# Queries and keys of the first heads projected side by side, some of their K tiles by seven products, in a two-layer hybrid decoder trunk

## The chip, the cores and the metric

The kernel runs on one core of a Trainium2 chip. The metric is the device time of one execution in microseconds (us); less is better. Engines are named as in the profile: PE is TensorE's matmul, PEld its weight load, DVE is VectorE, ACT is ScalarE, POOL is GpSimd, SP is SyncE, which issues most loads.

## The reference

Two layers, each on x of 256 tokens by 2048 columns, all in float32:

```python
h = _rmsnorm(x, attn_norm_g[l])
proj = h @ w_in[l]
q, k, v, gate_b, gate_c, conv_in = jnp.split(proj, splits, axis=-1)
q = _rmsnorm(q.reshape(B, S, N_HEADS, 2, HEAD_DK), q_norm_g[l])
k = _rmsnorm(k.reshape(B, S, N_HEADS, 2, HEAD_DK), k_norm_g[l])
...
conv = gate_b * _short_conv(gate_c * conv_in, conv_w[l])
x = x + jnp.concatenate([attn, conv.astype(attn.dtype)], axis=-1) @ w_out[l]
hm = _rmsnorm(x, mlp_norm_g[l]) @ w_up[l]
x = x + jnp.square(jax.nn.relu(hm)) @ w_down[l]
```

Each of the six parts of `proj` is 1024 columns wide. There are 8 heads of 128 value columns, and each head has two maps of 64 query and key columns: attention is the difference of two softmaxes, causal, with a relative bias. `w_up` is 2048 by 8192, `w_down` 8192 by 2048.

## The kernel before

**Number format.** A float32 product is made of three: every operand is split into a high part (ACT copies it, rounded, to the matmul's format) and a low part (DVE subtracts the high part from the whole), and high x high, high x low and low x high are accumulated (`TERMS`). So each weight tile costs one ACT operation and one DVE operation of 128x1024 (lines 328 and 329, tiles `whi` and `wlo`).

**Weights.** `Weights` holds a list of jobs in the order of use. `take()` hands out the next pair of parts, and builds three jobs ahead (`AHEAD`). A job loads 512 KB into one of four `raw` buffers (SP issues the load, line 369) and splits it into one of three `hi` and `lo` buffers. A job is a pair of K tiles (2 x 128 rows) by 512 columns.

**Order of the work.** PE's instructions run in the order of the program text; on the other engines the compiler orders the queue by a plan of its own, except for operations marked `late`, which keep program order. Work that lies beside the matmuls is written as generators in `Background`: every six matmuls or so `work.tick()` counts down their waits, and a piece whose wait is over issues its next operations, its transposes on PE among them. So "yield 12" is twelve ticks later.

**A layer.** `mixer` projects, for each half of the heads, q, k and v with `linear` (line 427): 8 jobs, 2 K tiles each, 2 token tiles, 3 terms, 96 matmuls of 128x512 a projection. `acc` is a tile of two PSUM banks, from a pool of two such tiles (`mm`); a further pool (`ps`) has three banks `bank` and one `av`, eight in all. After q, `qk_norm` (line 617) starts: for each token tile a square on ACT, a sum on DVE, the power on POOL (line 489), and the multiply into `wide` tiles on DVE (line 631); 12 ticks later the result is transposed on PE (line 640) and split by head (`q_parts`, `k_parts`). It runs under k's matmuls, k's norm under v's. `attention` of a half starts after its v and runs under what follows. Then come the convolution's gates (`linear_t`, `conv`), the output projection (`BySeven.left`, `.right`) and the MLP.

**The input norm.** `Norm.chunk` (line 502) transposes 512 columns of x on PE, multiplies by the gain and splits (`split_gained`, lines 294 and 296). There are four chunks, each of four K tiles, so pairs 6 and 7 of the eight pairs are chunk 3. The factors per row come later (`factors`, line 551): they are multiplied into the results, and a matmul with ones, "rbc" at line 578, lays them out along a row for the convolution.

**By seven products.** Two K tiles, two token tiles and two column chunks form a 2x2 by 2x2 block product, which is done here with seven products instead of eight (Winograd's form). `BySeven.sums_of` (line 797) makes the four sums of activations S1 to S4 (four DVE operations of 128x512, one ACT and one DVE to split), `jobs` (line 816) the parts of the weights in three jobs: `plain` loads two raw tiles and splits b11, b21 and b22; `sums` and `more` make and split t1, t3 and t2, t4. A product is three matmuls. Products 2, 3 and 4 go into the ordinary accumulators, 1, 5, 6 and 7 into banks of their own, which are gathered by ACT and DVE at the end (`results`, line 897). The output projection's right half does pairs 2 and 3 that way (order in `RIGHT`, `right()` at line 1003, line 876 for the matmuls), the down projection does 83 pairs (`quarters`, line 1165; `product`, line 1326), where `plain` splits 512 columns as `b1` and 1024 as `b2`.

**Bias.** `load_bias` (line 272) loads the reversed bias rows through POOL's queue (line 280) and copies them on ACT (line 286); in layer 0 it first runs the small setup (gains, lambda).

Of the kernel before, what the change touches and what calls it, by code (L numbers as in the profile page):

```python
# [15 lines left out]
P = 128  # L16
# [28 lines left out]
SEVEN_RIGHT = tuple(i for what, i in RIGHT if what == "s")  # L45

# [82 lines left out]
def trunk(ctx: ExitStack, tc: tile.TileContext, x, w_in, w_out, conv_w, q_norm_g, k_norm_g,  # L129
# [25 lines left out]
    work = Background()  # L155

# [115 lines left out]
    def load_bias(l, bpool, bias, setup):  # L272
# [219 lines left out]
    class Norm:  # L492
# [3 lines left out]
        def __init__(self, which, l):  # L496
            self.which, self.l = which, l
            self.squared = 0
            self.tiles = [Parts(apool, "a", f"nT{which}{l}_{n}") for n in range(D // CH)]
            self.ss = small.tile([P, NT, D // CH], F32, tag="ss", name=f"ss{which}{l}", bufs=2)  # L500

        def chunk(self, n, wait):
# [5 lines left out]
            for j in range(2):  # L508
                tp = bank(f"tpn{n}_{j}")
                for i in range(2):  # L510
                    k = 2 * j + i
                    for t in range(NT):
# [3 lines left out]
                split_gained(a, *((2 * j + i, tp[:, i * S:(i + 1) * S],  # L516
                                   norm_gain(self.which, self.l, n * KG + 2 * j + i))
                                  for i in range(2)))
# [32 lines left out]
        def factors(self):  # L551
# [24 lines left out]
            yield 5  # L576
# [40 lines left out]
    def qk_norm(acc, r, put, gain, name):  # L617

        out_ = []
        for t in range(NT):  # L620
            rt = r[:, t:t + 1]
            sq = wide(f"{name}sq{t}")
            nc.scalar.activation(sq, acc[:, t], AF.Square, scale=rt)
# [6 lines left out]
            qn = wide(f"{name}n{t}")  # L630
            nc.vector.tensor_tensor(
                qn.rearrange("p (g d) -> p g d", d=DK),
                acc[:, t].rearrange("p (g d) -> p g d", d=DK),
# [154 lines left out]
    class BySeven:  # L788
# [3 lines left out]
        def __init__(self, l, bpool, biasp, tmp, weights):  # L792
            self.l, self.pool, self.weights = l, bpool, weights
            self.biasp, self.tmp = biasp, tmp
            self.sums, self.rooms = {}, []

        def sums_of(self, i, a11, a21, a12, a22):

            if i < 4:
                if i % 2 == 0:  # L800
# [15 lines left out]
        def jobs(self, w, i, col):  # L816
# [3 lines left out]
            def split(hi, lo, src):  # L820
                nc.scalar.activation(hi, src, AF.Copy)
                nc.vector.tensor_sub(lo, src, hi.bitcast(F32))
# [7 lines left out]
            def plain():  # L830
                raws = []
                for n in range(2):
# [3 lines left out]
                               col + n * CH:col + (n + 1) * CH].rearrange(  # L836
# [9 lines left out]
            def sums():  # L846
                left, right = mine["raw"]
                pool, tag = (self.pool, "b") if col else (self.kpool, "kL")
# [30 lines left out]
        def pair(self, i, chunks, starts=(), last=False):  # L879

            for n, accs in chunks:
                hi, lo = self.weights.take()
                for j in range(2):
# [4 lines left out]
                    for t in range(NT):  # L888
                        for m, (pa, pw) in enumerate(TERMS):
                            nc.tensor.matmul(  # L890
                                accs[t], a.ap[:, pa, k % KG, t * P:(t + 1) * P],
                                (hi, lo)[pw][:, j],
                                start=(j == 0 and m == 0 and (n, t) in starts),
                                stop=(last and j == 1 and m == 2))
# [22 lines left out]
        def left_jobs(self, w_gate, col, w):  # L917

            weights, made = self.weights, {}
            for what, i in LEFT:  # L920
                if what == "c":
                    weights.jobs += weights.column(w_gate, col + i * P)
                elif what == "a":
                    made[i] = self.jobs(w, i, 0)
# [71 lines left out]
        def right_jobs(self, w):  # L996
            for what, i in RIGHT:
                if what == "s":
                    self.weights.jobs += self.jobs(w, i, 2 * CH)
                else:  # L1000
                    self.weights.plain(w, 2 * P * i, (2 + what) * CH, 2)

        def right(self, norm):
# [7 lines left out]
            def seven(i, start, end, rest):  # L1011
                if start:
                    for n in (1, 5, 6):
                        prods[n] = bank(f"po{l}r{n}")
                    prods[7] = ps.tile([P, CH], F32, tag="av", name=f"po{l}r7", bufs=1)
                b11, b21, b22 = weights.take()
                t1, t3 = weights.take()
                t2, t4 = weights.take()
                for n, a, b, chunk in ((1, A11, b11, None), (2, A12, b21, 0), (3, S4, b22, 1),
                                       (5, S1, t1, None), (7, S3, t3, None), (6, S2, t2, None),  # L1020
                                       (4, A22, t4, 0)):
                    if chunk is None:
                        self.product(n, i, a, b, start, end)
                    else:
                        self.product(n, i, a, b, False, not {"s", chunk} & rest)
                    if n == 5:
                        work.tick()
                work.tick()

            for j, (what, i) in enumerate(RIGHT):  # L1030
                rest = {w for w, _ in RIGHT[j + 1:]}
                if what == "s":
                    seven(i, i == SEVEN_RIGHT[0], i == SEVEN_RIGHT[-1], rest)
# [17 lines left out]
    def mixer(l, norm, loads):  # L1051

        with ExitStack() as scope:
# [9 lines left out]
            for half in range(2):  # L1063
                for part in range(3):
                    weights.straight(w_in[l], 0, D // P, part * AW + half * CH)
# [9 lines left out]
            bias = [biasp.tile([P, NH, S], F32, tag="bias", name=f"bias{j}") for j in range(2)]  # L1075
            work.start(load_bias(l, bpool, bias, setup), 10)
# [6 lines left out]
            for half in range(2):  # L1083
                h0 = 4 * half
                acc = linear(f"q{l}{half}", hT, weights)
                r = norm.r
                qT = bpool.tile([P, 2, 4, S], F32R, tag="b", name=f"qT{l}{half}")
                work.start(qk_norm(acc, r, q_parts(qT), q_gain[:, l:l + 1], f"q{l}{half}"))
                acc = linear(f"k{l}{half}", hT, weights)
                kT = bpool.tile([P, 2, 4, S], F32R, tag="b", name=f"kT{l}{half}")  # L1090
# [521 lines left out]
```

## Time and profile before

| what | value |
|---|---|
| median of 3 runs | 2118.36 us (2118.16 to 2118.75) |
| the profiled execution's own time | 2118.11 us |
| its span, first to last instruction | 2116.0 us |
| granted TensorE clock | 1.00 |
| DMA | 476.02 MB, mean 225 GB/s |
| loads of w_in | 191 of 512 KB, median 4.2 us to landing |

In the profile a group of instructions is given by line, engine, operation and tiles (out<-in). Timeline rows begin with the start in us from the span's start and the duration; several instructions in a row may be merged ("x6"). Rows of the chain in order of time have start, length and what ran. In a row of stages the pairs are busy us and the number of instructions for PE, PEld, DVE, ACT and POOL, then the granted clock, the DMA share and GB/s. Matmuls overlap in the trace (0.39 us each, one started every 0.23), so their pace is read from starts. First q matmul: 6.9 us in layer 0, 1063.1 in layer 1.

### The profile page before, as it was taken

What the parts mean: (1) busy time and instruction counts of PE and PEld (TensorE: products, weight loads), DVE (VectorE), ACT (ScalarE), POOL (GpSimd) and SP (SyncE); (2) the same over time, 40 slices, a digit from 0 to 9 for tenths busy, and PEclk for the clock granted to TensorE, in tenths of its full rate; (3) what the DMA queues carried; (4) which work ended last, traced back from release to release, by engine and by line L of the source; (5) the groups of instructions that cost most, each with busy time, mean ns of one, the idle gap of its engine ahead of it and who ended that gap; (6) DMA issues with size and microseconds to landing.
All of it is one profiled execution on the core that took longest, in us unless ns stands there. A gap on an engine that the chain in (4) does not pass through costs nothing.

```text
span 2116.0 us, 29387 instructions
## 1 busy us (share of the span) xinstructions
PE 2111.2 (100%) x10833; PEld 1804.9 (85%) x10833; DVE 1784.5 (84%) x2519; ACT 1401.8 (66%) x1880; POOL 159.4 (8%) x226
## 2 busy tenths in 40 slices
PE   9999999999999999999999999999999999999999
PEld 8888888888888888888888888888888888888887
DVE  6778788898888888799766788988988888888997
ACT  6777565676776776666566766557777677675664
POOL 3110100000000000011101101000000000000110
PEclk9999999999999999999999999999999999999999
DMA  8555665887777777788656555658877777777993
GB/s 280 175 154 179 186 193 189 288 258 229 236 230 231 229 238 229 248 299 293 213 170 181 165 171 180 207 179 291 258 229 238 230 236 229 231 229 262 318 311 104
DMA packets 313857, 476.02 MB, mean 225 GB/s; under 512 B 12692, under 2 KB 209638, under 8 KB 313713
## 3 DMA queue, kind: packets, MB, share of 16 engines
q1 hardware_dynamic: 285232, 406.76, 61.0%
q0 software_dynamic: 28288, 67.24, 10.0%
q8 instruction: 85, 1.39, 0.3%
q14 instruction: 60, 0.48, 0.1%
q10 hardware_dynamic: 192, 0.15, 0.0%
HBM read 440.52 MB, written 33.58 MB: 224 GB/s over the span
## 4 chain that ended last, share of the span: by engine, by line
PE 99%; ACT 0%; issue 0%; DMA 0%; DVE 0%
PE upc L1286 31%; PE pr L1329 14%; PE dn L1410 8%; PE ci L467 4%; PE gc L467 4%; PE gb L419 4%; PE k L442 4%; PE q L442 4%; PE v L442 4%; PE o L890 3%; PE dn L1504 2%; PE po L876 2%; PE dn L1329 2%; PE pr1r L1329 2%; PE po L890 2%; PE pr0r L1329 1%
## 5 line engine op out<-in xcount | busy, mean ns | idle before, releaser
L1286 PE MATMUL upc<-nT,uhi 128*128 128x512 f32 x1920 | 454.7, 389 | 0.0
L1286 PEld LDWEIGHTS upc<-nT,uhi 128*128 128x128 f32 x1920 | 360.3, 188 | 74.7
L1150 DVE TENSOR_TENSOR ulo<-uraw,uhi 128x1024 fp32r<-128x1024 f32 x256 | 311.9, 1222 | 110.8 <-ACT f L1318 90.8
L328 ACT ACTIVATE whi<-raw 128x1024 fp32r<-128x1024 f32 x246 | 260.0, 1059 | 211.4 <-PE v L442 22.1
L329 DVE TENSOR_TENSOR wlo<-raw,whi 128x1024 fp32r<-128x1024 f32 x246 | 298.5, 1222 | 118.1 <-ACT whi L328 85.7
L1149 ACT ACTIVATE uhi<-uraw 128x1024 fp32r<-128x1024 f32 x256 | 270.6, 1057 | 158.8 <-PE upc L1286 138.9
L1286 PEld LDWEIGHTS upc<-nT,ulo 128*128 128x128 f32 x1920 | 246.2, 191 | 9.3
L1286 PE MATMUL upc<-nT,ulo 128*128 128x256 f32 x1920 | 249.1, 283 | 0.0
L1410 PE MATMUL dn<-whi,fb 128*128 128x512 f32 x496 | 156.5, 389 | 0.0
L1175 ACT ACTIVATE b2h<-draw 128x1024 fp32r<-128x1024 f32 x83 | 88.2, 1062 | 48.5 <-PE pr L1329 39.8
L328 ACT ACTIVATE whi<-uraw 128x1024 fp32r<-128x1024 f32 x62 | 65.9, 1062 | 81.8 <-PE dn L1410 61.0
L1410 PEld LDWEIGHTS dn<-whi,fb 128*128 128x128 f32 x496 | 93.1, 188 | 19.2
L1296 ACT ACTIVATE ev<-upc 128x512 f32<-128x512 f32 x120 | 71.9, 599 | 53.4 <-PE upc L1286 53.4
L1175 ACT ACTIVATE t24h<-t 128x1024 fp32r<-128x1024 f32 x83 | 88.2, 1063 | 22.9 <-PE pr L1329 15.9
L1176 DVE TENSOR_TENSOR t24l<-t,t24h 128x1024 fp32r<-128x1024 f32 x83 | 101.2, 1220 | 1.7
L1176 DVE TENSOR_TENSOR b2l<-draw,b2h 128x1024 fp32r<-128x1024 f32 x83 | 101.1, 1218 | 1.1 <-ACT b2h L1175 1.1
L1176 DVE TENSOR_TENSOR t13l<-t,t13h 128x1024 fp32r<-128x1024 f32 x83 | 101.2, 1219 | 0.7
L1189 DVE TENSOR_TENSOR t<-draw 128x1024 f32<-128x1024 f32 x83 | 101.3, 1220 | 0.3
L1175 ACT ACTIVATE t13h<-t 128x1024 fp32r<-128x1024 f32 x83 | 88.3, 1064 | 13.3 <-DVE t L1189 2.9
L1410 PE MATMUL dn<-wlo,fb 128*128 128x512 f32 x248 | 96.5, 389 | 0.0
L1329 PE MATMUL pr<-t13h,f 128*128 128x512 f32 x240 | 93.8, 391 | 0.0
L329 DVE TENSOR_TENSOR wlo<-uraw,whi 128x1024 fp32r<-128x1024 f32 x62 | 75.8, 1223 | 17.9 <-ACT whi L328 17.6
(491 smaller groups left out, 4428.6 us busy)
## 6 DMA issues: line engine op xcount, KB each, us to landing
uraw<-in_w_up_dram SPq DMA_DIRECT2D x128, 1024.0 KB, 6.3
raw<-in_w_in_dram SPq DMA_DIRECT2D x191, 512.0 KB, 4.2
draw<-in_w_down_dram SPq DMA_DIRECT2D x174, 512.0 KB, 5.2
raw<-in_w_out_dram SPq DMA_DIRECT2D x64, 512.0 KB, 4.5
uraw<-in_w_down_dram SPq DMA_DIRECT2D x62, 512.0 KB, 5.9
raw<-in_w_down_dram SPq DMA_DIRECT2D x10, 1024.0 KB, 5.6
hid0p<-f POOLq DMA_DIRECT2D x19, 512.0 KB, 3.5
fb<-hid0p POOLq DMA_DIRECT2D x19, 512.0 KB, 6.8
```

The source lines that it names most:

```text
L328: pair = (nc.scalar.activation(hi, raw, AF.Copy), nc.vector.tensor_sub(lo, raw, hi.bitcast(F32)))
L329: nc.vector.tensor_sub(lo, raw, hi.bitcast(F32)))
L442: nc.tensor.matmul(acc[:, t], a.ap[:, pa, k % KG, t * P:(t + 1) * P], (hi, lo)[pw][:, j], start=(k == 0 and (pa, pw) == (0, 0)), stop=(k = ...
L467: nc.tensor.matmul(acc[:, f, 0] if part else acc[:, f], wt[:, k % 4, fs], a.ap[:, 0, k % KG] if part else a.ap[:, :, k % KG], start=(part ...
L890: nc.tensor.matmul(accs[t], a.ap[:, pa, k % KG, t * P:(t + 1) * P], (hi, lo)[pw][:, j], start=(j == 0 and m == 0 and (n, t) in starts), st ...
L1149: pair = (nc.scalar.activation(hi, src, AF.Copy), nc.vector.tensor_sub(lo, src, hi.bitcast(F32)))
L1150: nc.vector.tensor_sub(lo, src, hi.bitcast(F32)))
L1175: keep(nc.scalar.activation(hi, src, AF.Copy))
L1176: keep(nc.vector.tensor_sub(lo, src, hi.bitcast(F32)))
L1286: nc.tensor.matmul(acc[:, 0] if part else acc, wt[part][:, k], a.ap[:, 0, k % KG] if part else a.ap[:, :, k % KG], start=(part == 0 and kh ...
L1329: nc.tensor.matmul(prods[n], f[:, pa, a], b[pw], start=(start and m == 0), stop=(stop and m == 2))
L1410: nc.tensor.matmul(prods[p], f[:, pa, 2 * k + t], b[pw][:, n], start=(p in starts and k == 0 and m == 0), stop=(stop and k == 1 and m == 2))
```

## The change

For the first half of the heads, q and k are projected together by `BySeven.first`. It goes through the list `FIRST` of its layer: "(0, i)" is pair i for q, "(1, i)" for k, each 12 matmuls into that projection's two banks; "("s", i)" is pair i for both by seven products. Layer 0 does pair 7 by seven, layer 1 pairs 6 and 7. The products of their own take the three banks and `av`, so all eight are in use; meanwhile (`held`) the bias and the row factors' matmul wait. At the end of the last pair by seven, ACT and DVE gather products 1, 5, 6, 7 into five tiles; when a projection's last pair is done its accumulators are added to these, and `qk_norm` works on the sums in SBUF and multiplies in place. `Norm.chunk` makes the activation sums of those pairs, from a copy of the gained columns (two ACT operations of 256) that is then split at once (512). The weight parts `w7x` and `w7y` use the two `bias` buffers, so the bias tiles are allocated after them. The start of the bias in layer 1 moves from tick 10 to 20, the factors' matmul from 5 ticks behind the factors to 24. `seven` moves out of `right` and is shared. In the down projection, `quarters` splits b11, b21 and b22 in one operation of 1536 columns each on ACT and DVE, which needs the two column halves exchanged; accumulators and additions follow. The second half of the heads and all else stay as they are.

```diff
+FIRST = (((0, 0), (0, 1), (1, 0), (1, 1), (0, 2), (1, 2), (0, 3), (1, 3), (0, 4), (1, 4), ("s", 7), (0, 5), (1, 5), (0, 6), (1, 6)),
+         ((0, 0), (0, 1), (1, 0), (1, 1), (0, 2), (1, 2), (0, 3), (1, 3), ("s", 6), (0, 4), (1, 4), ("s", 7), (0, 5), (1, 5)))
...
+        while held:
+            yield 1
+        bias += [biasp.tile([P, NH, S], F32, tag="bias", name=f"bias{j}") for j in range(2)]
...
+                    y = wide(f"ny{pair}").rearrange("p (k s) -> p k s", k=2)
+                    for i in range(2):
+                        nc.scalar.activation(y[:, i], tp[:, i * S:(i + 1) * S], AF.Copy,
+                                             scale=scales[i])
+                    hi, lo = (a[:, part, 2 * j:2 * j + 2] for part in range(2))
+                    nc.scalar.activation(hi, y, AF.Copy)
+                    nc.vector.tensor_sub(lo, y, hi.bitcast(F32))
+                    self.sums_of(pair, *(y[:, i, t * P:(t + 1) * P]
+                                         for i in range(2) for t in range(NT)))
...
-            yield 5
+            yield 24
+            while held:
+                yield 1
...
-            qn = wide(f"{name}n{t}")
+            qn = acc[t] if in_place else wide(f"{name}n{t}")
...
+                pair = (nc.scalar.activation(hi, src, AF.Copy),
+                        nc.vector.tensor_sub(lo, src, hi.bitcast(F32)))
+                if self.rooms_of == 8:
+                    for ins in pair:
+                        late(ins)
...
+            for j, (what, i) in enumerate(FIRST[l]):
+                rest = {w for w, _ in FIRST[l][j + 1:]}
+                if what == "s":
+                    while not self.cat[2 * i // KG].ready:
+                        work.tick()
+                    held.append(i)
+                    self.seven(i, i == SEVEN_FIRST[l][0], i == SEVEN_FIRST[l][-1], rest)
+                    if i == SEVEN_FIRST[l][-1]:
+                        held.clear()
+                        room = self.tmp.tile([P, 2, CH], F32, tag="ao", name="qe", bufs=1)
+                        e1, e2, e3 = room[:, 0], wide("qe2"), room[:, 1]
+                        e4, e5 = (self.tmp.tile([P, CH], F32, tag="s", name="ke", bufs=2)
+                                  for _ in range(2))
+                        nc.scalar.activation(e1, prods[1], AF.Copy)
+                        nc.vector.tensor_add(e2, prods[6], e1)
+                        nc.vector.tensor_add(e4, prods[5], e2)
+                        nc.vector.tensor_add(e3, prods[7], e2)
+                        nc.vector.tensor_add(e5, prods[5], e3)
+                        e = ((e1, e3), (e4, e5))
+                else:
+                    starts = [(what, t) for t in range(NT) if what not in opened]
+                    opened.add(what)
+                    self.pair(i, [(what, accs[what])], starts, not {"s", what} & rest)
+                for n in list(left):
+                    if not {"s", n} & rest:
+                        for t in range(NT):
+                            nc.vector.tensor_add(e[n][t], accs[n][t], e[n][t])
+                        done(n, e[n])
+                        left.remove(n)
...
-            work.start(load_bias(l, bpool, bias, setup), 10)
+            work.start(load_bias(l, bpool, biasp, bias, setup), 20 if l else 10)
...
-                    h1, l1 = parts(raw[:, 0, 0], "b1", 1)
-                    h2, l2 = parts(raw[:, 1], "b2", 1)
-                    return (h1, l1), (h2[:, 0], l2[:, 0]), (h2[:, 1], l2[:, 1])
+                    raw = mine["raw"] = load_rows(i, col).rearrange("p k (n c) -> p (k n) c", n=2)
+                    h, lw = parts(raw[:, 1:4], "b", 1)
+                    return tuple((h[:, m], lw[:, m]) for m in (0, 2, 1))
...
-                    for n, t, p in ((0, 0, 2), (0, 1, 4), (1, 0, 3), (1, 1, 8)):
+                    for n, t, p in ((1, 0, 2), (1, 1, 4), (0, 0, 3), (0, 1, 8)):
```

More of the change, by code (lines that the diff above doesn't have):

```diff
@@ L1009, in right @@
             opened, add = set(), None
[L1011 to L1028, printed above, removed]
             for j, (what, i) in enumerate(RIGHT):
@@ L1062, in mixer @@
                 setup = setup_loads(bpool.tile([P, 2 * KG * S], F32, tag="b", name="setup"))
-            for half in range(2):
-                for part in range(3):
-                    weights.straight(w_in[l], 0, D // P, part * AW + half * CH)
+            qk_first = BySeven(l, bpool, biasp, tmp, weights, 8)
+            qk_first.cat = norm.tiles
+            norm.sums_of = qk_first.sums_of
+            qk_first.first_jobs(w_in[l])
+            for half, part in ((0, 2), (1, 0), (1, 1), (1, 2)):
+                weights.straight(w_in[l], 0, D // P, part * AW + half * CH)
             for q in range(AW // WC):
@@ L1386, in seven_onto @@
             def seven_onto(n):
-                x11, x21, x12, x22 = (xs[n + i][:, t] for i in range(2) for t in range(NT))
+                x11, x21, x12, x22 = (xs[n + 1 - i][:, t] for i in range(2) for t in range(NT))
                 e1, e2, e3, e4 = wide("e1"), wide("e2"), wide("e3"), wide("e4")
```

122 lines of the change are left out of this document (84 added, 38 removed).

## The prediction

> **What bounds the kernel now.** I read the page first, then who waited for whom on PE, then the chain of work in order of time around the first heads of each layer.
>
> ```profile
> span 2116.0 us, 29387 instructions
> PE 2111.2 (100%) x10833; PEld 1804.9 (85%) x10833; DVE 1784.5 (84%) x2519; ACT 1401.8 (66%) x1880; POOL 159.4 (8%) x226
> PE 99%; ACT 0%; issue 0%; DMA 0%; DVE 0%
> PE warm L183 <- DVE mhalf L175: 1.1, 1, 1.1
> ```
>
> The third line is the chain that ended last: it is PE throughout. The fourth is the whole answer on PE's waits: one wait of 1.1 us, before anything is computed. So PE never waits, and the time is the number of matmuls times their pace. A change pays here only by having fewer matmuls, and costs only by making PE wait. A busy PE need not be at its pace, so I check that in the stage that is changed and in the stage that already works by seven products.
>
> ```profile
> 1086.52 16.32 PE k L442 x72
> ```
>
> ```profile
> 355.83 0.84 PE L876 MATMUL po0r<-w7b,cat 128*128 128x512 f32 x3
> ...
> 359.23 0.84 PE L876 MATMUL po0r<-w7y,sf 128*128 128x512 f32 x3
> ...
> 360.59 0.39 PE L890 MATMUL o<-whi,cat 128*128 128x512 f32 x1
> ```
>
> The k projection of layer 1: 16.32 us / 72 = 0.2267 us for a 128x512 matmul. One pair of K tiles by seven in the output projection goes from 355.83 to 360.59, 4.76 us for 21 matmuls: 0.2267 as well. Both forms run at the same pace, without gaps.
>
> The profiled execution took 2118.11 us with a span of 2116.0, so 2.11 us lie around the span and stay. It is 0.25 below the median of the runs shown (2118.36). All sums below are made against 2118.11; against the median everything is 0.25 higher.
>
> **What the change removes.** A pair of K tiles for one chunk is 2 tiles x 2 token tiles x 3 terms = 12 matmuls; for q and k together 24. By seven products it is 7 x 3 = 21. Layer 0 does one such pair, layer 1 two: 3 x 3 = 9 matmuls less, 9 x 0.2267 = **2.04 us**. Every other matmul and transpose stays, some in another place. PE is never covered by anything, so these 2.04 us come off the end if no new wait appears: 2116.07. The question is whether DVE, ACT and the banks let PE go through.
>
> **What it adds on DVE.** I take start-to-start distances in a full queue:
>
> ```profile
> 328.22 0.69 DVE L907 TENSOR_TENSOR es<-po,e 128x512 f32<-128x512 f32 x1
> 328.82 0.68 DVE L908 TENSOR_TENSOR x<-po,x 128x512 f32<-128x512 f32 x1
> ...
> 611.00 1.22 DVE L1319 TENSOR_TENSOR f<-h,f 128x1024 fp32r<-128x1024 f32 x1
> 612.13 1.22 DVE L1150 TENSOR_TENSOR ulo<-uraw,uhi 128x1024 fp32r<-128x1024 f32 x1
> ```
>
> 0.60 us for 512 columns, 1.13 for 1024. A pair by seven needs three lo parts of 1024, one of 512 and four sums of 512: 3 x 1.13 + 5 x 0.60 = 6.4 us, in place of two plain lo parts (2.26): 4.1 more. The sums of its activations are five operations of 512, 3.0 us. Collecting the products (four operations) and adding them to the accumulators (four): 4.8 us a layer. Norming in place has as many operations as before. Where two gained lo parts of 256 (an estimated 0.35 each, by the same rows) become one of 512, 0.1 goes. Layer 1: 2 x 4.1 + 2 x 3.0 + 4.8 - 0.2 = 18.8 us; layer 0: 4.1 + 3.0 + 4.8 - 0.1 = 11.8.
>
> ```profile
> 22.00:45.00 23.00, 23.00 (x105) 18.21 (x104) 16.30 (x31) 13.87 (x26) 5.63 (x8) 1.00 0.80 275
> 45.00:77.00 32.00, 32.00 (x150) 26.52 (x149) 20.50 (x25) 23.23 (x32) 7.56 (x6) 1.00 0.62 183
> 1063.00:1085.00 22.00, 22.00 (x103) 18.17 (x101) 12.70 (x20) 11.38 (x17) 1.52 (x3) 1.00 0.60 170
> 1085.00:1099.00 14.00, 14.00 (x63) 11.62 (x62) 9.70 (x12) 10.52 (x15) 3.66 (x4) 1.00 0.67 194
> 1099.00:1124.00 25.00, 25.00 (x115) 20.70 (x115) 16.53 (x20) 14.16 (x17) 3.67 (x4) 1.00 0.62 186
> ```
>
> The columns are PE, PEld, DVE, ACT, POOL. Layer 1 has 12.70 + 9.70 + 16.53 = 38.9 us of DVE in 61; with 18.8 more, 57.7 in about 59.6, or 97%. Layer 0: 36.8 + 11.8 = 48.6 in 54, 90%. So in layer 1 DVE comes to within 2 us of the stage's length. Does the kernel already hold that somewhere?
>
> ```profile
> 346.00:367.00 21.00, 20.40 (x28) 1.00 0.63 196
> ```
>
> ```profile
> 356.48 1.22 DVE L822 TENSOR_TENSOR w7y<-w7t,w7y 128x1024 fp32r<-128x1024 f32 x1
> ```
>
> Yes: in the output projection's two pairs by seven DVE is busy 20.40 of 21 us (97%), and PE does not wait; the last part w7y is done at 357.7, 1.5 us before its first matmul at 359.23. That is 21 us and not 60, but the new stage spreads the load: the activation sums are asked for early in layer 1 and needed only 20 us later.
>
> How late may a split be?
>
> ```profile
> 1081.12 1.06 ACT L328 ACTIVATE whi<-raw 128x1024 fp32r<-128x1024 f32 x1 [1.66 <-PE q L442]
> ```
>
> ```profile
> 1082.21 1.23 DVE L329 TENSOR_TENSOR wlo<-raw,whi 128x1024 fp32r<-128x1024 f32 x1 [1.50 <-ACT whi L328]
> ```
>
> A split starts when PE gives back one of three buffers, two groups of 12 (2.72 us each) before the k group at 1086.52 that uses it, and is done at 1083.44: 3.1 us of cover. I count DVE's work by deadline in layer 1, from the first q matmul on. The first pair by seven comes after eight groups of 2.72 us and a little over 0.8 of transposes, its product 5 at 24.6. By then DVE owes six splits (6.8), the row factors (1.0), chunk 3 (1.2), one set of sums (3.0) and the pair's b, t and x parts (4.1): 16.1 of the 23.1 us it has from 1.5 on. At the second pair's last part the same count gives 30.1 of 34.7, at the k transposes about 55 of 58. No deadline is missed; the last one is close.
>
> **Norms side by side.** Both norms now start within 2.7 us and run under v.
>
> ```profile
> 1090.32 1.64 POOL L489 TENSOR_TENSOR q_r<-q_e,mhalf 128x8 f32<-128x8 f32 x1
> ```
>
> Four of these are 6.6 us of POOL, in 16.3 us (12 ticks of six matmuls) from the end of a projection to its transposes: hidden.
>
> ```profile
> 1103.85 2.79 ACT L597 ACTIVATE qT<-q10tp,q_gain 64x512 fp32r<-64x512 f32 x4
> ```
>
> On ACT these four head splits of q (0.70 us each) and the eight of k now follow each other, and layer 1's eight bias copies (512 columns, at most as long: 5.6) move 10 ticks later, beside the squares. ACT has 10.84 us free of 25 in the last row of the windows, where q's splits stand already; the bias fits. If that cover went, PE would wait at a transpose, 1 to 3 us. What else is moved: the two reversed-bias loads of layer 1 on POOL's queue go from tick 10 to 20, behind the row factors and ahead of the norms' powers, and are needed at tick 32 or later; the broadcast of the row factors (0.43 us on PE) moves, its readers come in the convolution. SP issues the same bytes in another order; the pair by seven holds two of the four raw buffers until its last sum.
>
> ```profile
> 359.38 0.69 DVE L851 TENSOR_TENSOR w7t<-raw 128x512 f32<-128x512 f32 x1 [0.55 <-DMA raw<-in_w_out_dram]
> ```
>
> That cost DVE 0.55 us in the output projection and PE nothing. I take nothing for all these; the upper bound is in the rivals.
>
> **The banks.** The pair by seven fills all eight banks, and v's accumulator is q's old one. Its nearest row is the end of the output projection:
>
> ```profile
> 370.56 0.68 DVE L906 TENSOR_TENSOR e<-po0r,es 128x512 f32<-128x512 f32 x1
> ...
> 376.43 1.29 DVE L1044 TENSOR_TENSOR x<-o,x 128x512 f32<-128x512 f32 x2 [0.40 <-PE o L890]
> ```
>
> Four collecting operations of 0.60 begin as the last product ends; two adds begin 0.40 us after their group's end and take 1.2. In the new code k's last group (2.72 us) lies between q's end and v's start: 1.6 us of adds fit with 1.1 to spare, just one split (1.13) between them. Below zero this cannot go: PE had no wait here to lose.
>
> **The down projection's merged split.** 83 times a 512 and a 1024 split become one of 1536, behind product 3.
>
> ```profile
> 604.54 1.06 ACT L1175 ACTIVATE b2h<-draw 128x1024 fp32r<-128x1024 f32 x1 [0.74 <-PE pr L1329]
> ...
> 938.09 1.06 ACT L1175 ACTIVATE b2h<-draw 128x1024 fp32r<-128x1024 f32 x1 [0.41 <-PE dn L1329]
> ```
>
> ```profile
> 618.16 0.40 PE L1329 MATMUL pr<-b1h,f 128*128 128x512 f32 x1
> ...
> 946.05 0.39 PE L1329 MATMUL pr0r<-b1h,fb 128*128 128x512 f32 x1
> ```
>
> From b2h's start my estimate is 1.5 us on ACT and 1.7 on DVE, so it is ready near 607.9 and 941.5, 10 and 4.5 us before use. No cost; and as PE does not wait there, no gain either. The exchange of the two column halves changes no count.
>
> **The sum.** 2118.11 - 2.04 = 2116.07, plus a wait. The unknown wait lies between 0 (the output projection, the nearest row) and 5.3 (rival 2). I take 0.6, half a split late at layer 1's k transposes, where DVE has least to spare: **2116.7 us**. What a measurement can tell from no change is about 0.2%, 4.2 us: the whole expected gain is half of that.
>
> **Rivals.**
>
> 1. *The evacuation takes the place of what was saved.* If two splits stand in DVE's queue before q's adds, v waits 1.6 + 2.26 - 2.72 = 1.1 us in each layer: 2116.07 + 2.3 = **2118.4**, no change. For it: a queue in fixed order, 97% load. Against: the rows at 376.43. The Trainium skill, Perfetto Trace Analysis, section Matmuls, advises letting matmul groups rotate through different PSUM banks so that evacuating one overlaps the next group; taking all eight banks for two projections speaks against this change. The trace before, with the same eight banks in use at 355 to 371, shows no wait, so by the trace it holds only if the adds are late.
>
> 2. *DVE's order makes the splits late (slower).* The place is layer 1 after chunk 3 of the norm: two sums of 3.0 us and two 0.60 lo parts, 7.2 us, ahead of one split with 3.1 us of cover: 4.1 us. In layer 0 one sum, one lo part and the chunk's two gained ones: 3.0 + 0.6 + 0.7 - 3.1 = 1.2. Together 5.3: **2121.4**, slower by 3.3. It decides from the point where more than 3.1 us of other work stands ahead of a split. Against it: needed late, they can be placed late.
>
> 3. *More than counted goes.* Only half as many norm chunks are asked for at a given time, so the start of each layer is less tight. PE shows no wait there, only a slower pace at the kernel's start:
>
> ```profile
> 6.98 4.46 PE q L442 x18
> ...
> 12.32 5.46 PE q L442 x24
> ```
>
> 18 matmuls are 4.08 us at 0.2267, so 0.38 is lost there, and 0.02 in the next 24: **2115.7** if all of it came back.
>
> 4. *The change doesn't pay at all*: something else paces the stage, and 2118.1 stays. Against it is PE's empty list of waits.
>
> **How the numbers follow.** Forecast (2115.9 to 2117.7): 0.60. Rival 1, with late norms (2117.7 to 2119.5): 0.18. Rival 2 (2119.5 to about 2124): 0.14. Rival 3: 0.04. Rival 4: 0.04. The range 2115.6 to 2121.2 leaves out part of rivals 2 and 3, some 0.1. Faster by over 0.2% (under 2114.1) needs more than all that is known to be lost here: 0.02. Slower by over 0.2% (over 2122.6) is rival 2 with the same lateness more than once: 0.08. Within: 0.90.
>
> **What would show it.** Right: PE's list of waits stays near 1.1 us, q and k run at 0.2267, and the first v matmul follows k's last by 0.23 us in both layers. Rival 1 shows as a PE wait at v's first matmul on an add; rival 2 as PE waits on wlo, w7x or w7y with DVE busy before them. A PE wait at the k transposes on the norm's multiply would be the 0.6. I am wrong if the down projection's pairs wait for their b part, or if PE shows no wait and the time is still off by over 1 us.

## The result and the profile after

| | before | after |
|---|---|---|
| median (lowest to highest) of 22 runs each, same chip | 2118.66 us (2118.0 to 2119.53) | 2121.35 us (2119.56 to 2123.46) |
| ratio, 95% interval | | 1.0013 (1.0007 to 1.0019) |
| the profiled execution's own time | 2118.11 us | 2121.82 us |
| its span | 2116.0 us | 2120.1 us |

The changed kernel is slower by 2.7 us, 0.13%. The forecast was 2116.7, the range ended at 2121.2. The head of the page of after, then the whole answer on PE's waits (us in total, times, longest):

```profile
span 2120.1 us, 29191 instructions
PE 2110.3 (100%) x10824; PEld 1802.1 (85%) x10824; DVE 1803.7 (85%) x2482; ACT 1395.7 (66%) x1811; POOL 162.1 (8%) x226
```

```profile
PE q L449 <- DVE wlo L336: 2.1, 2, 1.1
PE k L919 <- DVE wlo L336: 1.4, 1, 1.4
PE warm L187 <- DVE mhalf L179: 1.1, 1, 1.1
PE gb L426 <- ACT gb L798: 0.6, 1, 0.6
PE q L919 <- ACT whi L361: 0.4, 1, 0.4
PE po0r L902 <- DVE w7y L845: 0.3, 1, 0.3
```

PE has its 9 matmuls fewer (10833 to 10824), and where before only the wait at "warm" stood, five more stand now. Three of them are for a low part from DVE (`wlo`, `w7y`).

To place the loss, the span is cut at the first matmul of each stage on PE, read from the timeline of both traces. All stages not in the table (k and v of the second heads, the convolution, the output projection, both MLPs) agree within 0.02 us.

| stage, from first matmul to first matmul (us) | before | after | after less before |
|---|---|---|---|
| up to the first q matmul | 6.91 | 6.76 | -0.15 |
| layer 0, first heads: q, k, v | 72.18 | 72.85 | +0.67 |
| layer 0, second heads: q ("q01") | 24.20 | 25.17 | +0.97 |
| layer 0, gate beside the output projection ("gb") | 84.82 | 85.11 | +0.29 |
| layer 1, first heads: q, k, v | 68.63 | 69.01 | +0.38 |
| layer 1, second heads: q ("q11") | 24.17 | 25.16 | +0.99 |
| layer 1, gate ("gb") | 84.81 | 85.69 | +0.88 |

The sum is +4.03; PE's last matmul starts 4.04 us later than before (the 0.01 left is in the stages not shown). The execution's own time grew by only 3.71: around the span lie 2.11 us before and 1.72 after. The first heads hide what they saved: 3 matmuls (0.68 us) in layer 0 and 6 (1.36) in layer 1. So they lost 1.35 and 1.74 us, the second heads' q 0.97 and 0.99, the gate stages 1.17 together.

**The first heads.** In layer 1, the timelines of PE, ACT, DVE and POOL of after:

```profile
1086.75 0.50 PE L919 MATMUL k<-wlo,nT 128*128 128x512 f32 x1 [1.43 <-DVE wlo L336]
```

```profile
1079.75 1.06 ACT L335 ACTIVATE whi<-raw 128x1024 fp32r<-128x1024 f32 x1 [1.71 <-PE q L919]
```

```profile
1084.27 0.69 DVE L877 TENSOR_TENSOR w7t<-raw 128x512 f32<-128x512 f32 x1 [4.97 <-DMA raw<-in_w_in_dram]
1084.88 0.69 DVE L878 TENSOR_TENSOR w7t<-raw 128x512 f32<-128x512 f32 x1
1085.48 1.22 DVE L336 TENSOR_TENSOR wlo<-raw,whi 128x1024 fp32r<-128x1024 f32 x1
```

Read them from the bottom up. PE waits 1.43 us for a plain pair's `wlo`. Its input, the `whi`, was ready at 1080.81 (1079.75 + 1.06). But DVE's queue holds two sums of the pair by seven ahead of it, and the first of these waits for its load: DVE stands idle for 4.97 us with ready work behind. The load is late because of what was issued beside it:

```profile
1070.57 1.87 POOL L284 DMA_DIRECT2D rev<-by_dist_d  x2 [1.69 <-PE tpn L521]
```

```profile
q0 software_dynamic: 504, 1.93, 48.9%
q1 hardware_dynamic: 814, 1.57, 36.9%
...
raw<-in_w_in_dram SPq DMA_DIRECT2D x3, 512.0 KB, 7.6
```

The second fence is the DMA view of 1074 to 1085 us: the reversed-bias rows (two loads of 1 MB on POOL's queue, q0) move 1.93 MB while SP's queue q1, with the weights, moves 1.57, and a weight load takes 7.6 us. The same window of before has no q0:

```profile
q1 hardware_dynamic: 1059, 2.04, 62.2%
...
raw<-in_w_in_dram SPq DMA_DIRECT2D x4, 512.0 KB, 3.7
```

There the bias loads had gone out before the layer began:

```profile
1035.28 1.82 POOL L280 DMA_DIRECT2D rev<-by_dist_d  x2 [5.05 <-issue]
```

The Trainium skill, DMA: Bandwidth & Descriptors, section Issuing engines are not separate DMA queues, says that transfers started from different engines run on the same 16 DMA engines and interleave. The rows agree: with POOL's queue active, a load on SP's queue takes 7.6 us in place of 3.7 (the median of three loads, and of four). Layer 0 shows the same pattern: DVE's `w7t` there waits 2.91 us for its load, beside bias loads issued at 26.39. PE shows it as the wait of 0.29 for `w7y` and a few gaps of under 0.5 around the pair by seven.

```profile
33.59 0.69 DVE L877 TENSOR_TENSOR w7t<-raw 128x512 f32<-128x512 f32 x1 [2.91 <-DMA raw<-in_w_in_dram]
```

**The second heads' q.** ACT in layer 1 of after, at the last of k's head splits, and PE:

```profile
1129.65 0.68 ACT L631 ACTIVATE kT<-k10tp,gains 64x512 fp32r<-64x512 f32 x1
...
1134.54 0.69 ACT L632 ACTIVATE kT<-k10tp,gains 64x512 fp32r<-64x512 f32 x1
1135.24 2.01 ACT L335 ACTIVATE whi<-raw 128x1024 fp32r<-128x1024 f32 x2
```

```profile
1138.08 0.50 PE L449 MATMUL q<-wlo,nT 128*128 128x512 f32 x1 [1.06 <-DVE wlo L336]
```

Two plain `whi` stand behind eight head splits of k (5.6 us), and q's four came just before those, with one `whi` between. The hi parts, the lo part behind them and PE are late: 1.06 us of wait. Before, q's head splits lay 20 us earlier, under k's projection (they end at 1106.64, k's begin at 1126.55). k's eight stood in the same place as now, and the hi parts behind them began at

```profile
1132.13 2.01 ACT L328 ACTIVATE whi<-raw 128x1024 fp32r<-128x1024 f32 x2
```

That is 0.36 us after the first q11 matmul (1131.77), and the gap on PE was 0.25. In after it is 1.32 us behind it (1133.92): 0.96 later, and the stage is 0.99 longer.

### The profile page after: what moved, and what is told of

It is laid out like the page before. It is cut to its first block, busy times and chain, and to the rows that moved or that the text cites. A ratio compares the mean times of both kernels' runs of the same rounds, so it can differ in the third digit from the quotient of the medians.

```text
span 2120.1 us, 29191 instructions
## 1 busy us (share of the span) xinstructions
PE 2110.3 (100%) x10824; PEld 1802.1 (85%) x10824; DVE 1803.7 (85%) x2482; ACT 1395.7 (66%) x1811; POOL 162.1 (8%) x226
## 4 chain that ended last, share of the span: by engine, by line
PE 96%; DMA 1%; ACT 1%; DVE 1%; issue 1%; POOL 0%; ACTq 0%; DVEq 0%; POOLq 0%
PE upc L1376 31%; PE pr L1419 14%; PE dn L1500 8%; PE ci L474 4%; PE gc L474 4%; PE gb L426 4%; PE v L449 3%; PE o L919 3%; PE dn L1594 2%; PE dn L1419 2%; PE k L449 2%; PE q L449 2%; PE po L902 2%; PE pr1r L1419 2%; PE po L919 2%; PE pr0r L1419 1%
## 5 line engine op out<-in xcount | busy, mean ns | idle before, releaser
L335 ACT ACTIVATE whi<-raw 128x1024 fp32r<-128x1024 f32 x240 | 253.5, 1059 | 194.0 <-issue 20.6
L336 DVE TENSOR_TENSOR wlo<-raw,whi 128x1024 fp32r<-128x1024 f32 x240 | 290.7, 1221 | 90.2 <-ACT whi L335 58.0
L1266 ACT ACTIVATE bh<-draw 128x1536 fp32r<-128x1536 f32 x83 | 123.9, 1493 | 97.6 <-PE pr L1419 80.7
L1267 DVE TENSOR_TENSOR bl<-draw,bh 128x1536 fp32r<-128x1536 f32 x83 | 146.0, 1758 | 12.0 <-ACT bh L1266 11.3
L1419 PE MATMUL pr<-bh,f 128*128 128x512 f32 x360 | 121.4, 391 | 0.0
```

Of the source, the lines that this page charges most:

```text
L335: pair = (nc.scalar.activation(hi, raw, AF.Copy), nc.vector.tensor_sub(lo, raw, hi.bitcast(F32)))
L336: nc.vector.tensor_sub(lo, raw, hi.bitcast(F32)))
L1266: keep(nc.scalar.activation(hi, src, AF.Copy))
L1267: keep(nc.vector.tensor_sub(lo, src, hi.bitcast(F32)))
L1419: nc.tensor.matmul(prods[n], f[:, pa, a], b[pw], start=(start and m == 0), stop=(stop and m == 2))
```

## The experiments

Three edits to the changed kernel take one suspected cost each: K puts k's head splits 3 ticks later, R1 puts layer 1's bias loads ahead of the layer, R0 puts layer 0's setup and bias loads 6 ticks later. Each ran alone and in all combinations. Each of the twelve kernels of this part ran 11 times, beside the kernel before; the interval of one ratio is about 0.0009 to each side, 1.9 us. So the medians alone don't separate single cures, and each verdict also goes by the stage's length in the profile, which for an undisturbed stage repeats to 0.05 us.

| kernel | median us | ratio to before, 95% interval | first heads' q and k, layer 0 / 1 | q01 / q11 |
|---|---|---|---|---|
| before (2118.66 to 2118.86) | | | 49.48 / 45.92 | 24.20 / 24.17 |
| after | 2121.35 | 1.0013 (1.0007, 1.0019) | 48.73 / 45.34 | 25.17 / 25.16 |
| all plain | 2120.79 | 1.0010 (1.0001, 1.0019) | 48.11 / 44.98 | 25.20 / 25.17 |
| all plain, K | 2118.11 | 0.9996 (0.9987, 1.0005) | 48.09 / 44.98 | 23.79 / 23.80 |
| before, merged split only | 2118.11 | 0.9998 (0.9989, 1.0007) | 49.48 / 45.92 | 24.20 / 24.17 |
| before, q beside k | 2120.61 | 1.0009 (1.0000, 1.0018) | 48.55 / 44.98 | 25.18 / 25.17 |
| K | 2118.94 | 1.0002 (0.9993, 1.0011) | 48.76 / 44.41 | 23.82 / 23.80 |
| R1, copies late | 2121.48 | 1.0015 (1.0006, 1.0024) | 48.59 / 43.62 | 25.17 / 26.21 |
| R1 | 2120.38 | 1.0009 (1.0000, 1.0017) | 49.53 / 43.62 | 25.18 / 25.19 |
| R0 | 2121.80 | 1.0013 (1.0004, 1.0022) | 47.40 / 45.38 | 25.18 / 25.20 |
| K, R1 | 2118.57 | 1.0001 (0.9992, 1.0010) | 49.59 / 43.61 | 23.82 / 23.80 |
| K, R0 | 2117.48 | 0.9995 (0.9986, 1.0004) | 47.38 / 43.80 | 23.82 / 23.80 |
| R0, R1 | 2119.06 | 1.0002 (0.9993, 1.0011) | 47.74 / 43.62 | 25.15 / 25.21 |
| K, R0, R1 | 2116.28 | 0.9987 (0.9978, 0.9996) | 47.63 / 43.62 | 23.81 / 23.80 |

In the fourth column the rows "before" and "merged split only" don't compare with the others: elsewhere q's transposes lie under v and not under k, 0.95 us in each layer.

### All pairs plain

```diff
-FIRST = (((0, 0), ... ("s", 7), (0, 5), (1, 5), (0, 6), (1, 6)), (... ("s", 6), (0, 4), (1, 4), ("s", 7), ...))
+FIRST = (((0, 0), (0, 1), (1, 0), (1, 1), (0, 2), (1, 2), ... (0, 6), (1, 6), (0, 7), (1, 7)),) * 2
-                            nc.vector.tensor_add(e[n][t], accs[n][t], e[n][t])
+                            nc.vector.tensor_copy(e[n][t], accs[n][t])
```

> The changed kernel with all eight pairs of K tiles of both layers' first heads plain (no pair by seven; q and k side by side, norms in place, order of the work and the merged split as changed). It issues 9 matmuls more than the changed kernel, as many as the kernel before. Theory A (three separate losses: the pairs by seven lose 2.7 us at the first stages because their raw loads land late; k's head splits standing right behind q's on ACT lose 1.9 us at the stages of q01 and q11; the gate stages lose 0 to 1.2): the time before plus 1.9 to 3.1, that is 2120.6 to 2121.8, with PE's waits at the first q and k stages for wlo gone and the one at q01 (1.2 us) still there. Rival B (DVE or ACT is simply overloaded by the sums of the pairs by seven, and all losses come from there): 2118.4 to 2119.0, and the loss at q01 goes too.

Measured 2120.79. PE's waits for the pairs by seven are gone, and the one at q01 and q11 stays to the last digit:

```profile
PE q L449 <- DVE wlo L336: 2.1, 2, 1.1
```

```profile
PE q L448 <- DVE wlo L335: 2.1, 2, 1.1
```

The first is after, the second all plain (its lines are shifted by one). So the loss at q01 and q11 has nothing to do with the seven products; it comes with side by side alone. Theory A holds, rival B falls.

### The down projection's part alone

```diff
-                    h1, l1 = parts(raw[:, 0, 0], "b1", 1)
-                    h2, l2 = parts(raw[:, 1], "b2", 1)
+                    h, lw = parts(raw[:, 1:4], "b", 1)
```

> The kernel before with only the down projection's part of the change (one split of 1536 columns in place of 512 and 1024, and the column halves exchanged). Theory: no part of the 2.7 us comes from it: 2118.7, within 0.4 of the kernel before. Rival: it delays the pairs by seven of the MLP or the evacuation at its end: 2119.2 or more.

Measured 2118.11, and both MLP stages have the length of before (681.11 and 677.53 us). The merged split costs nothing. The median is 0.67 under that of before beside it (2118.78), more than the 0.4 expected; half of that is the time around the span, which is 1.77 us here and 2.11 before (means over the runs).

### Layer 1's bias loads ahead (R1), in two forms

```diff
-            work.start(load_bias(l, bpool, biasp, bias, setup), 20 if l else 10)
+            work.start(load_bias(l, bpool, biasp, bias, setup), 0 if l else 10)
-        yield 4 if l else 12
+        yield 32 if l else 12
```

> The changed kernel with layer 1's reversed-bias loads issued at the layer's start (before the row factors on POOL's queue, as in the kernel before), the bias copies kept at tick 32. Theory (the two loads of 1 MB each collide with the raw loads of the pair by seven, which then land 3 us late, and DVE's queue stands behind them): PE's wait for wlo in layer 1's first stage goes, the first stage of layer 1 gets 1.3 to 1.7 us shorter, 2119.6 to 2120.1 in all. Rival (the four raw buffers or DVE's own load set the pace, and the loads' collision is a bystander): 2121.0 to 2121.7, with the wait still there.

Measured 2121.48: as the rival had it, though the stage did what the theory said. Layer 1's q and k took 43.62 us and not 45.34, PE's wait there was gone, but q11 went from 25.16 to 26.21. The cause was the edit: with 32 ticks the bias copies came later than in the changed kernel, right ahead of q's head splits on ACT (layer 1):

```profile
1124.55 1.14 ACT L293 ACTIVATE bias<-rev 128x512 f32<-128x512 f32 x2
1125.60 2.78 ACT L619 ACTIVATE qT<-q10tp,q_gain 64x512 fp32r<-64x512 f32 x4
```

The second form has `yield 24 if l else 12`, which leaves ACT's order as changed.

> The earlier experiment with layer 1's reversed-bias loads ahead, mended: there the bias copies had come 8 ticks later than in the changed kernel and pressed on q's head splits on ACT; here they stand where the changed kernel has them, and ACT's order is the changed kernel's. Theory (in the earlier run the first stage's gain of 1.72 us was given back by those copies at q11, 1.05 us, the rest being the landing of the gate stages' loads, which differs from execution to execution): the first stage of layer 1 is 43.6 us, q11's stage is again 25.1 to 25.2, 2119.5 to 2120.2 in all. Rival (whatever is won in the first stage is lost behind it, because the loads and not the splits set the pace of the layer): 2121.0 to 2121.8.

Measured 2120.38, a little above the theory's band and below the rival's; first heads 43.62, q11 25.19, as the theory said. With the loads gone, the pair's own load landed in 4.1 us (the window of 1074 to 1085 again):

```profile
q1 hardware_dynamic: 837, 1.60, 45.3%
...
raw<-in_w_in_dram SPq DMA_DIRECT2D x4, 512.0 KB, 4.1
```

All five kernels with the loads ahead have 43.61 or 43.62 in layer 1, which is the all-plain stage less 6 matmuls: 44.98 - 1.36 = 43.62. The kernels without it have 45.34, 44.41, 45.38 and 43.80. So the collision costs 0.2 to 1.8 us, as the loads happen to land, and moving the loads takes away all of it. The size follows from DVE's wait at `w7t`: it is 4.97, 4.04, 4.99 and 3.42 us in these four kernels, and each time 3.2 us more than what the stage lost (1.72, 0.79, 1.76, 0.18). With the loads ahead the wait is 1.7 to 1.8 us and costs nothing. So about 3.2 us of lateness is covered, as the prediction had read from the trace before (3.1).

### k's head splits later (K)

```diff
-        yield 12
+        yield wait          # 15 for k of the first half, else 12
-                                     1 + half, by_seven.sums_of), 1 + 9 * half)
+                                     1 + half, by_seven.sums_of), 1 + 9 * half + 3 * (half == 0))
```

> The changed kernel with k's transposes and head splits for the first half 3 ticks later, in both layers, so that other hi parts stand between q's four head splits and k's eight on ACT (the attention of that half starts 3 ticks later as well). Theory (twelve head splits in a row delay a plain pair's hi part, and PE loses 1 us in each of the two stages q01 and q11): those two stages get 0.8 to 1.0 us shorter each, 2119.4 to 2119.8 in all. Rival (the loss there is what the first stages' lateness has left over, or the head splits only move the wait into the stage after): 2121.0 to 2121.8.

Measured 2118.94, below the theory's band, and q01 and q11 at 23.82 and 23.80. Now, on ACT in layer 1, a plain hi part stands in the middle of k's eight:

```profile
1132.21 0.69 ACT L632 ACTIVATE kT<-k10tp,gains 64x512 fp32r<-64x512 f32 x1
1132.92 1.06 ACT L335 ACTIVATE whi<-raw 128x1024 fp32r<-128x1024 f32 x1
1134.01 0.69 ACT L1186 ACTIVATE v<-v,rowf 128x512 fp32r<-128x512 f32 x1
1134.59 0.67 ACT L631 ACTIVATE kT<-k10tp,gains 64x512 fp32r<-64x512 f32 x1
```

The stages are 1.35 us shorter, not the 0.8 to 1.0 expected; 0.3 a layer of that only moves to the stages behind (the convolution grows by 0.2, v by 0.1).

### The converse: before, with q's head splits beside k's

```diff
-                work.start(qk_norm(acc, r, q_parts(qT), q_gain[:, l:l + 1], f"q{l}{half}"))
+                work.start(qk_norm(acc, r, q_parts(qT), q_gain[:, l:l + 1], f"q{l}{half}",
+                                   12 if half else 26))
```

> The converse: the kernel before with q's transposes and head splits of the first half 14 ticks later, so that ACT's order there is the changed kernel's (four of q, one hi part, eight of k, two hi parts); nothing else of the change. Theory: the stages q01 and q11 lengthen from 24.2 to 25.1 or 25.2 us each, 2120.4 to 2120.9 in all (before plus 1.9). Rival (the loss at q01 and q11 belongs to the side-by-side order or to the pairs by seven): 2118.6 to 2119.2 and those stages at 24.2.

Measured 2120.61; q01 25.18, q11 25.17, and the wait of after stands in a kernel that has nothing else of the change:

```profile
PE q L442 <- DVE wlo L329: 2.1, 2, 1.1
```

### All plain, with K

The first experiment's edit and K together.

> The all-plain kernel of the first experiment (no pair by seven in the first heads, 9 matmuls more than changed) with k's head splits 3 ticks later. Theory (the neighbourhood of q's and k's head splits on ACT is all that side by side costs without the pairs by seven): 2120.79 less 1.9, that is 2118.5 to 2119.2, the time of the kernel before. Rival (something else of the new order costs as well): 2119.8 to 2120.9.

Measured 2118.11, at the time of before and 0.4 under the band's lower end. So the head splits' neighbourhood is all that side by side costs.

### Layer 0's setup and bias loads later (R0)

```diff
-            work.start(load_bias(l, bpool, biasp, bias, setup), 20 if l else 10)
+            work.start(load_bias(l, bpool, biasp, bias, setup), 20 if l else 16)
```

> The changed kernel with layer 0's small setup and its two reversed-bias loads started 6 ticks later (tick 16 in place of 10), so that they no longer go out beside the raw loads of the pair by seven at 25 us. Theory (the collision delays those loads by 3 us, and PE pays 1.1 us for it in layer 0): the first stage of layer 0 (first q to first v) gets 0.5 to 1.0 us shorter than its 48.7 us, 2120.4 to 2120.9 in all. Rival (the lateness there has another cause, such as the start's own loads): stage unchanged within 0.2, 2121.0 to 2121.7; or the loads collide with the next raw loads, and the wait only moves.

The stage did what the theory said (47.40 in place of 48.73), the median didn't: 2121.80, above the theory and just above the rival's band. By itself this run decides nothing. The stage repeats in the three combinations below: 47.38, 47.74, 47.63, against 48.59 to 49.59 in the five kernels with the pair by seven and the loads as changed.

### The combinations

> The changed kernel with two cures: layer 1's reversed-bias loads ahead (bias copies where they were) and k's transposes and head splits of the first half 3 ticks later in both layers. Theory (the two losses are separate and add): 2118.94 less 1.7, that is 2116.9 to 2117.6, faster than the kernel before by 1 to 2 us. Rival (they share one cause, so the second cure brings nothing): 2118.6 to 2119.3.

Measured 2118.57, at the edge of the rival's band; the stages, however, have both gains (43.61, and 23.82 and 23.80).

> The changed kernel with k's head splits 3 ticks later (both layers) and layer 0's setup and reversed-bias loads 6 ticks later; layer 1's loads as changed. Completes the combinations of the three cures. Theory (three separate losses): 2118.94 less 1.0 to 1.3, that is 2117.4 to 2118.2, with layer 0's first stage at 47.4 to 47.7 us and layer 1's q11 stage at 23.8. Rival (the later loads of layer 0 bring nothing by themselves, as the one run with them alone, 2121.80, says): 2118.7 to 2119.5.

Measured 2117.48, as the theory had it; layer 0's first heads at 47.38, q11 at 23.80.

> The changed kernel with both layers' reversed-bias loads moved (layer 0 later, layer 1 ahead), k's head splits as changed. Theory: the kernel with all three cures (2116.28) plus the 1.9 us of the head splits: 2117.9 to 2118.6, first stages at 47.4 to 47.7 and 43.6 us. Rival (the cures help only together): 2119.5 or more.

Measured 2119.06, between theory and rival.

> The changed kernel with all three cures: layer 1's reversed-bias loads ahead, k's head splits 3 ticks later, and layer 0's setup and reversed-bias loads 6 ticks later. Theory (three separate losses of 1.7, 1.9 and 0.5 to 1.0 us): 2116.0 to 2117.0, which is what the 9 matmuls fewer (2.04 us) leave of the kernel before, with 0 to 0.4 us of waits and some lateness of the gate stages' loads. Rival: as the run with two cures or slower.

Measured 2116.28, ratio 0.9987 (0.9978 to 0.9996): faster than both kernels. With the eight combinations, each cure can be averaged over four kernels with and four without it: K 2117.82 against 2120.65, **-2.8 us**; R1 2118.57 against 2119.89, **-1.3**; R0 2118.66 against 2119.81, **-1.2**. The sum is 5.3, the whole step from after to all three 5.07. That the three losses add is not shown by these sums, in which the effect of one cure on another cancels, and single medians scatter (R0 is +0.45 by itself and -2.29 beside K and R1). It is shown by the stages: each cure shortens its own stage with the others or without them. In the stages from the first q matmul to the gate, the kernel with all three is 2.17 us shorter than before (245.32 against 245.90 and 240.71 against 242.30). That this is near the 2.04 us of the 9 matmuls is luck: all plain with K, which has as many matmuls as before, is already 0.49 shorter than before (245.65 and 242.06), its q01 and q11 being 0.4 shorter each. The pairs by seven give the other 1.68.

## Why the prediction was wrong, point by point

**Right: what is removed.** 9 matmuls, at 0.2267 us each. Beside all plain with K, which has q and k side by side as well, the kernel with all three cures is 1.35 us shorter in layer 1 (6 matmuls are 1.36) and 0.33 in layer 0 (3 are 0.68); in the profile with K and R0, layer 0 is 0.70 shorter.

**Not quite right: "PE never waits."** The list of waits has nothing for before at q11, but its timeline has the gap of 0.25 there. The kernels with K bring q01 and q11 0.4 us under those of before.

**Failed: "I take nothing for all these."** Two of the things costed at nothing were the loss.

- *The bias loads.* The prediction listed them ("the two reversed-bias loads of layer 1 on POOL's queue go from tick 10 to 20") and asked only when they were needed ("at tick 32 or later"; the copies that read them are started at tick 24). It should have asked beside what they would now run: 2 MB in the 10 us in which the pair by seven's first loads are due. It quoted a row of such a load being late by 0.55 us at no cost; here DVE stood 4.97 us. Measured: 1.3 us over the combinations. In layer 0 the loads were not moved; the pair by seven moved beside them, 1.2 us more.
- *ACT's head splits.* "ACT has 10.84 us free of 25 ...; the bias fits" is an average over 25 us. The next plain hi part is due within about 3 us, and stood behind 5.6 us of k's head splits with q's just ahead. The text had the price of a lost cover (1 to 3 us), but looked for it at a transpose; it was at the first low part of the next projection, 1.0 a layer by the stages, 2.8 in all by the combinations (of which before had 0.4 a layer as well).

**Failed: "2.11 us lie around the span and stay."** After has 1.76 on average, and so (1.76 to 1.80) has every kernel with the merged split, also where it stands alone; before and "before, q beside k" have 2.10. This gain of 0.3 hid a part of the loss. The runs do not show why. The least difference that a measurement can tell was also put too high: the interval above is 0.06% to each side, not 0.2%.

**The 0.6 at layer 1's k transposes** did not show: no such wait is in the list.

**Rival 1 (the evacuation) fell.** In both layers v's first matmul follows k's last by 0.23 us (55.49 after 55.26, 1110.25 after 1110.02), as the prediction's own sign asked. q's adds were ready with 0.8 us to spare:

```profile
1108.79 0.68 DVE L1097 TENSOR_TENSOR qe<-q,qe 128x512 f32<-128x512 f32 x1
```

They end at 1109.47, v begins at 1110.25. So taking all eight banks, which the prediction held against the change, cost no wait here.

**Rival 2 gave the time (2121.4 against 2121.35), but not for its reason.** It expected splits late behind 7.2 us of DVE work. Its sign was "PE waits on wlo ... with DVE busy before them"; the waits are there, but in layer 1's first heads DVE was idle before the late part, waiting for a load, and the loss at q01 and q11, 1.96 us by the stages, began on ACT. Its size was wrong as well. The sums of activations (and the text on the kernel before) are not operations of 128x512:

```profile
1071.77 0.28 DVE L834 TENSOR_TENSOR sv<-ny 128x128 f32<-128x128 f32 x1
1071.97 0.28 DVE L832 TENSOR_TENSOR sv<-ny 128x128 f32<-128x128 f32 x1
```

That is 0.20 us from start to start and not 0.60, so a set takes 4 x 0.20 + 0.60 = 1.4 us and not 3.0. The rival's 7.2 us become 4.0, 0.9 over the cover, nothing is left of it in layer 0, and its time becomes 2117.0: that 2121.4 came out is luck. Nor was DVE's load the limit. In the kernel with all three cures, the same 61 us of layer 1 have DVE busy for 52.28 (third pair of the row, after PE and PEld), 86%, where the prediction counted 57.7 and 97% (3.2 of the difference are the two sets of sums); and PE is busy all through:

```profile
1063.00:1124.00 61.00, 61.00 (x278) 50.53 (x277) 52.28 (x77) 39.55 (x54) 12.86 (x11) 1.00 0.59 184
```

**The merged split** cost PE nothing, as predicted; its 1.5 us on ACT were right:

```profile
606.31 1.50 ACT L1266 ACTIVATE bh<-draw 128x1536 fp32r<-128x1536 f32 x1 [1.47 <-PE pr L1419]
```

**Left open.** In the profiled execution the gate stages lost 1.17 us more: ACT's queue there waits for a load of the output projection, 3.84 us where before it was 2.58, and `gb` is copied out late.

```profile
1337.32 1.06 ACT L844 ACTIVATE w7b<-raw 128x1024 fp32r<-128x1024 f32 x1 [3.84 <-DMA raw<-in_w_out_dram]
```

```profile
1332.92 1.06 ACT L821 ACTIVATE w7b<-raw 128x1024 fp32r<-128x1024 f32 x1 [2.58 <-DMA raw<-in_w_out_dram]
```

The instructions there stand in the same order in both kernels. The profiles of the changed family lose 0.7 to 2.9 us in the two gate stages, those of before and its two variants at most 0.15. But the medians ask for little of it: without the gate stages the table above gives +2.86 us for after, less 0.34 around the span +2.52, and the median is +2.69; for q beside k, whose time around the span is that of before, the same sum is +1.84, the median +1.75. Whether ordinary executions have this loss was not settled. Nor was DVE's order tried by itself (the low part ahead of the sums, with the loads left late), and R0 moves layer 0's small setup with the loads, so that the two are not told apart.

## What to carry to other kernels

When an edit moves a transfer, ask what it runs beside and not only when it is needed; and when it adds an instruction that waits for a load to an in-order queue, count the load's worst landing, since all that is ready behind it waits too. Look up the shape of an operation before a rival is priced by it. Free time on an engine, taken over a stage, says nothing about a block of work that stands in one piece ahead of a part with 3 us of cover. A gain of 0.1% can be had back by moving such blocks a few ticks: three edits to wait counts brought this change from 2.7 us slower to 2.5 us faster.

## What was not expected of the hardware

Bias loads of 2 MB on POOL's queue, beside weight loads of 512 KB on SP's, took 48.9% of the DMA engines' time against 36.9%, and the weight load went from 3.7 to 7.6 us; no row shows the loads that PE was waiting for being let ahead. How late a load lands differed from kernel to kernel under such contention, so that one stage took 43.80, 44.41, 45.34 or 45.38 us with the same instructions in it; without it the same stage took 43.61 or 43.62 five times. After's 22 runs spread over 3.9 us, the 22 of before beside them over 1.5.
